# Splitting the weights of a two-layer encoder by DMA instead of on ScalarE and VectorE

## The chip, the cores and the metric

The kernel runs on one core of one Trainium2 chip. The metric is the device time of one execution in microseconds (us), the median of several runs. The engines are named as in the profile: PE is TensorE's matmul, PEld its weight load, DVE is VectorE, ACT is ScalarE, POOL is GpSimd, SP is SyncE. SPq, ACTq and POOLq are the instruction queues from which these three engines issue DMAs; q1 is the DMA queue that SP's transfers use and q0 the one that POOL's use.

## What is computed

Two request groups, 512 and 256 tokens of 1024 features in float32, go through the same two encoder layers:

```
n = rmsnorm(x)
q, k, v, xr, yr, g = split(n @ w_in)            # w_in is 1024 x 7168
att = rmsnorm(diff_attention(rope(norm(q)), rope(norm(k)), v))
rec = (scan_forward + scan_backward)(conv(xr)) * gelu(yr)
x   = x + (sig(g0) * (att @ w_a) + sig(g1) * (rec @ w_r)) @ w_out
x   = x + square(relu(rmsnorm(x) @ w_ff1)) @ w_ff2   # 1024 -> 4096 -> 1024
```

All products are wanted to float32 accuracy. TensorE takes the type float32r, which keeps the upper part of a float32. So each operand is split into an upper part hi (rounded to float32r) and a lower part lo = x - hi, and each product is three matmuls: hi by hi, hi by lo, lo by hi.

## The kernel before

The 768 tokens lie along the free axis, the features on the 128 partitions, 8 tiles of them. The weights come from HBM as 304 strips over the two layers: 288 of 128 x 1024 float32 (512 KB) and 16 of 128 x 512 (`rgw`, the gates of the recurrence). The list `plan` (from line 206) holds them in the order in which PE takes them. `prefetch(upto)` (line 225) issues for each strip of the plan a load on SP's queue into `raw` (2 buffers), then `split`: ACT rounds `raw` into `whi` (line 197) and DVE subtracts it into `wlo` (line 200). `whi` and `wlo` have WB = 4 buffers each. `wload` (line 239) hands PE its strip and has the strips up to AHEAD = 8 further on prefetched, as far as buffers allow.

The order of PE's instructions is the order of the program. For the other engines and the queues a planner fixes the order at build time: it places every instruction when its inputs and buffers are free by its own estimates. On the chip each engine and each queue then runs in that fixed order, so an instruction that waits holds up all that stand behind it.

A layer has four stages. In the attention stage (about 395 us) PE takes projections of q, k, v and a gate, 32 strips, and between their chunks, at places written out in the table STEPS, the steps of the 8 heads: transposes, scores, softmax on ACT and DVE, products with v. In the branch stages (`wa`, `wr`) the first four strips (NF = 4) are used together, feature tile by feature tile, in `first_strips`. Between them lies the recurrent stage, whose convolution and scans are ACT's and DVE's. The feed-forward stage (about 540 us) takes 64 strips one after the other.

POOL issues few transfers: stores of attention results (`ats`, line 634) and their loads (line 690), stores and loads of the branch sums (`ms`, lines 707 and 835), loads and stores of x (lines 856 and 925). It also adds the branch sums (line 842). The loads of x for layer 0 are issued on SP's queue (lines 371 and 373), between them the first two weight strips.

Of the kernel before, what the change touches and what calls it, by code (L numbers as in the profile page):

```python
# [9 lines left out]
F32 = mybir.dt.float32  # L10
F32R = mybir.dt.float32r
AF = mybir.ActivationFunctionType
ALU = mybir.AluOpType
# [16 lines left out]
AHEAD = 8  # strips of weights that are split ahead of their use  # L30
# attention: how many chunks of the other products (FILL, in this order) the tensor engine takes before each step of
# each of the 8 heads
# [23 lines left out]
# recurrent tiles in pairs: x: input and convolution, y: output gate, g: gates of the recurrence (tile, direction),  # L56
# s: scan, d: a strip of the branch's gate
# [6 lines left out]
WB = 4  # strips of split weights on chip  # L64

# columns of the packed per-feature vectors
V_N1, V_N2, V_BG, V_CW, V_CB, V_RB, V_RL, V_SG, V_GQ, V_GK, NV = 0, 8, 16, 32, 64, 72, 104, 120, 121, 122, 123
# columns of the vectors that every partition holds
# [4 lines left out]
def trunk_kernel(ctx: ExitStack, tc: tile.TileContext, xT, wqk, wv, wx, wy, wg0, wg1, wa, wr, wo, wf1, wf2,  # L73
# [10 lines left out]
    ident = cp.tile([P, P], F32, name="ident")  # L84
    make_identity(nc, ident)
    # the mean over D on every partition; over the 128 features of a head it is 8 times that
# [19 lines left out]
    def small_params(l, ap_):  # L106
        """per-layer scalars: -lam, 8 softplus(-L), folded gains, rotary tables."""
        v_ = vt[l]
        r_ = ap_.tile([P, NR], F32, name=f"rep{l}", tag="rep")
        nc.scalar.dma_start(out=r_, in_=rep[l])  # L110
        o = {}
        lam_init = 0.8 - 0.6 * math.exp(-0.3 * l)
        o["sg"] = tiny([P, 1], f"sg_{l}", "sg")
        V.tensor_scalar(out=o["sg"], in0=v_[:, V_SG:V_SG + 1], scalar1=-4.0 * (1.0 - lam_init), scalar2=0.0,
                        op0=ALU.mult, op1=ALU.add)
        o["gs"] = tiny([P, 1], f"gs_{l}", "gs")
        V.tensor_tensor(out=o["gs"], in0=v_[:, V_GQ:V_GQ + 1], in1=v_[:, V_GK:V_GK + 1], op=ALU.mult)
        # lam
        pr = tiny([P, 2, HD], f"lpr_{l}", "lpr")
        lv = r_[:, R_LV:R_LV + 256].rearrange("p (a b d) -> p a b d", a=2, b=2)  # L120
        V.tensor_tensor(out=pr, in0=lv[:, :, 0, :], in1=lv[:, :, 1, :], op=ALU.mult)
        ls = tiny([P, 2], f"ls_{l}", "ls")
        V.reduce_sum(out=ls, in_=pr, axis=AX)
        fn("ln_exp", ls, ls, AF.Exp)
        o["nlam"] = tiny([P, 1], f"nlam_{l}", "nlam")
        V.tensor_tensor(out=o["nlam"], in0=ls[:, 1:2], in1=ls[:, 0:1], op=ALU.subtract)
        V.tensor_scalar(out=o["nlam"], in0=o["nlam"], scalar1=1.0, scalar2=-lam_init, op0=ALU.mult, op1=ALU.add)
        # rotary tables with the gains: [P, NT, 4, ROT]
        o["t1"] = ap_.tile([P, NT, 4, ROT], F32, name=f"t1_{l}", tag="t1")
        o["t2"] = ap_.tile([P, NT, 4, ROT], F32, name=f"t2_{l}", tag="t2")  # L130
        for nm, c0, w in (("t1", R_GC, 0), ("t2", R_GS, 1)):
            V.tensor_tensor(
                out=o[nm], in0=rott[:, w].unsqueeze(2).to_broadcast([P, NT, 4, ROT]),
                in1=r_[:, c0:c0 + 64].rearrange("p (c d) -> p c d", c=4).unsqueeze(1).to_broadcast([P, NT, 4, ROT]),
                op=ALU.mult)
        # 8 softplus(-L) = 8 (max(-L, 0) + log1p(exp(-|L|)))
        L_ = v_[:, V_RL:V_RL + 16]
        mx = tiny([P, 16], f"spm_{l}", "spm")
        ng = tiny([P, 16], f"spn_{l}", "spn")
        V.tensor_scalar(out=ng, in0=L_, scalar1=-1.0, scalar2=0.0, op0=ALU.mult, op1=ALU.add)  # L140
        V.tensor_scalar(out=mx, in0=ng, scalar1=0.0, scalar2=0.0, op0=ALU.max, op1=ALU.add)
        e_ = tiny([P, 16], f"spe_{l}", "spe")
        V.tensor_tensor(out=e_, in0=L_, in1=ng, op=ALU.min)
        fn("ln_exp", e_, e_, AF.Exp)
        s_ = tiny([P, 16], f"sps_{l}", "sps")
        V.tensor_scalar(out=s_, in0=e_, scalar1=1.0, scalar2=2.0, op0=ALU.mult, op1=ALU.add)
        V.reciprocal(out=s_, in_=s_)
        V.tensor_tensor(out=s_, in0=s_, in1=e_, op=ALU.mult)
        s2 = tiny([P, 16], f"spq_{l}", "spq")
        V.tensor_tensor(out=s2, in0=s_, in1=s_, op=ALU.mult)  # L150
        pl = tiny([P, 16], f"spp_{l}", "spp")
        NS = 8
        V.tensor_scalar(out=pl, in0=s2, scalar1=1.0 / (2 * NS + 1), scalar2=1.0 / (2 * NS - 1), op0=ALU.mult, op1=ALU.add)
        for i in range(NS - 2, -1, -1):
            V.tensor_tensor(out=pl, in0=pl, in1=s2, op=ALU.mult)
            V.tensor_scalar(out=pl, in0=pl, scalar1=1.0, scalar2=1.0 / (2 * i + 1), op0=ALU.mult, op1=ALU.add)
        V.tensor_tensor(out=pl, in0=pl, in1=s_, op=ALU.mult)
        V.scalar_tensor_tensor(out=pl, in0=pl, scalar=2.0, in1=mx, op0=ALU.mult, op1=ALU.add)
        o["sp"] = tiny([P, 16], f"sp_{l}", "sp")
        o["nsp"] = tiny([P, 16], f"nsp_{l}", "nsp")  # L160
        V.tensor_scalar(out=o["sp"], in0=pl, scalar1=8.0, scalar2=0.0, op0=ALU.mult, op1=ALU.add)
        V.tensor_scalar(out=o["nsp"], in0=pl, scalar1=-8.0, scalar2=0.0, op0=ALU.mult, op1=ALU.add)
        return o

# [4 lines left out]
    def table(name):  # L169
        """what follows uses another table set of ScalarE than what came before: keep the two apart."""  # L170
# [23 lines left out]
    def split(hi, lo, src, eng="act"):  # L194
        """src (f32, SBUF) = hi + lo exactly."""
# [6 lines left out]
    # the weights in the order in which the tensor engine takes them; they are loaded and split ahead of it  # L202
# [22 lines left out]
    def prefetch(upto):  # L225
        while len(ready) < min(upto, len(plan)):
# [5 lines left out]
            raw = wp.tile([P, n], F32, tag="raw", name=nm("raw"), bufs=2)  # L232
            nc.sync.dma_start(out=raw, in_=src)
            hi = wp.tile([P, n], F32R, tag="whi", name=nm("whi"), bufs=WB)
            lo = wp.tile([P, n], F32R, tag="wlo", name=nm("wlo"), bufs=WB)
            split(hi, lo, raw)
# [10 lines left out]
    def mm3(ps, pairs):  # L247
        """pairs: (weight hi, weight lo, x hi, x lo) per k-tile; stationary is the first pair."""
# [6 lines left out]
    def strip(ps_pool, w, acts, g):  # L255
        """one strip of 128 output features for the tokens of group g."""
# [7 lines left out]
    def first_strips(ps_pool, name, l, acts):  # L264
        """the first strips of a branch side by side, k-tile by k-tile: the last tiles of acts come late"""
# [14 lines left out]
    def newton(vv, y, q, out=None, add=0.0, f=1.0):  # L280
        """y = ln(v / f + add) -> -2 f rsqrt(v / f + add) in out (q by default)."""
# [8 lines left out]
    def prep(xt, gm, nh, nl, g, k):  # L290
        """x * gain, split; the norm's factor is applied to the products."""
# [6 lines left out]
    def squares(xt, g, alloc, before=None):  # L298
        """sum over the feature tiles of x^2, split"""
# [16 lines left out]
    def stats(ss, rb, rtok, g, alloc, ps_pool, ptag, np_pool=None, ntag=None):  # L316
        """rb = -2 / rms of the tokens on every partition; rtok = 1 / rms with the tokens on partitions."""
# [23 lines left out]
    def scaled(out, ps, rb, g):  # L341
        """out = ps / rms"""
        off, n = GROUPS[g]
        V.scalar_tensor_tensor(out=out, in0=ps, scalar=-0.5, in1=rb[:, off:off + n], op0=ALU.mult, op1=ALU.mult)  # L344
# [7 lines left out]
    def norm1(l, xt, alloc):  # L352
        """splits x * gain for the two groups and sums the squares; the rest follows beside the first products"""
# [25 lines left out]
    for l in range(DEPTH):  # L379
        v_ = vt[l]  # L380
        # ================= attention =================
# [9 lines left out]
        def tok_proj(w, t, j, c):  # L391
            """token tile t, 256 columns of chunk c of w -> half a bank."""
# [14 lines left out]
        def proj_out(h, tp, ps, rtok):  # L407
            """the products of two token tiles, times 1 / rms; their squares per component"""
# [8 lines left out]
        def proj_close(h):  # L417
            """norms of q and k, rotary embedding"""
# [40 lines left out]
        def proj_first():  # L459
            """head 0, group A, k-tile by k-tile as the input comes"""  # L460
# [67 lines left out]
        def core(h):  # L528
            """steps of one head, each a function that issues one batch for the tensor engine and what follows it."""
# [3 lines left out]
            def tr_qk(g, w):  # L533
# [10 lines left out]
                # component c lies in the rows r; q's lower part and a second copy of k's upper part go to the rows o  # L544
# [14 lines left out]
            def score(qt):  # L559
# [8 lines left out]
                # (qh + ql) kh over all rows, qh kl over the half of the rows in which the component lies  # L568
# [20 lines left out]
            def tr_w(qp, kp):  # L589
                """qp: pair of query tiles (0, 1 of group A; 2 of B); kp: pair of key tiles"""  # L590
# [59 lines left out]
        # the norm's factors are worked out while the first products run  # L650
# [32 lines left out]
        # ================= attention branch =================  # L683
# [26 lines left out]
        # ================= RG-LRU =================  # L710
# [9 lines left out]
        def rg_x(j):  # L720
            """input of the recurrence: product, convolution, split"""
# [95 lines left out]
        # ================= recurrent branch, merge =================  # L817
# [34 lines left out]
        # ================= output projection =================  # L852
# [21 lines left out]
        # ================= feed-forward =================  # L874
# [8 lines left out]
        for c in range(NC_):  # L883
# [10 lines left out]
            for s, g in order:  # L894
# [3 lines left out]
                if c == 0 and s < 2:  # L898
                    # the norm's factors come while the first two strips run
# [32 lines left out]
        # the pools of this half are closed before the next layer's attention opens its own  # L932
# [80 lines left out]
```

## Time and profile before

| | us |
|---|---|
| median of 3 runs (2759.18 to 2762.40) | 2761.06 |
| span of the profiled execution | 2757.5 |
| PE busy in it | 2727.5 (99%) |
| PEld busy | 2430.3 (88%) |
| DVE busy | 1638.4 (59%) |
| ACT busy | 1323.3 (48%) |
| POOL busy | 96.5 (3%) |

The profiled execution gives its own time as the span, from the first to the last instruction; the median lies 3.6 us above it. Matmuls overlap in the records, so the mean duration of a matmul is longer than the time between two of them. An engine's busy share is a mean over stages with different limits.

### The profile page before, as it was taken

How to read it: one execution, taken by the hardware profiler on the slowest of the kernel's cores; microseconds unless marked ns; L12 is line 12 of the kernel's file. 1: busy time of each engine (PE TensorE's matmuls, PEld its weight loads, DVE VectorE, ACT ScalarE, POOL GpSimd, SP SyncE). 2: the span in 40 equal slices, each digit the busy share in tenths (PEclk: the TensorE clock that was granted, in tenths of full speed). 3: DMA queues.
4: the chain of work that ended last, by engine and by line, in shares of the span. 5: the costliest groups of instructions: out<-in, count | busy, mean ns of one | idle time of the engine just before them, and what ended most of it. 6: DMA issues, size and time to landing. Idle time of an engine off the chain costs nothing.

```text
span 2757.5 us, 41112 instructions
## 1 busy us (share of the span) xinstructions
PE 2727.5 (99%) x16840; PEld 2430.3 (88%) x16840; DVE 1638.4 (59%) x2966; ACT 1323.3 (48%) x2293; POOL 96.5 (3%) x134
## 2 busy tenths in 40 slices
PE   8999999999999999999999999999999999999999
PEld 8899888888888888888898988888888888888888
DVE  8777873697645444444567778637985454444443
ACT  7777871568324222222467778716683242222221
POOL 0000000000120000000100000000002100000000
PEclk9999999999999999999999999999999999999999
DMA  3111123122331111111321111231213222112111
GB/s 129 53 49 54 44 86 122 60 65 69 117 103 65 62 62 66 65 62 62 103 69 45 46 57 45 98 107 54 73 64 141 80 66 65 62 62 69 62 62 69
DMA packets 57485, 199.36 MB, mean 72 GB/s; under 512 B 7504, under 2 KB 9936, under 8 KB 57296
## 3 DMA queue, kind: packets, MB, share of 16 engines
q1 hardware_dynamic: 48384, 161.50, 17.9%
q0 software_dynamic: 8192, 34.61, 3.5%
q8 instruction: 132, 2.16, 0.3%
q10 hardware_dynamic: 720, 0.62, 0.1%
q14 instruction: 57, 0.47, 0.1%
HBM read 177.83 MB, written 18.87 MB: 71 GB/s over the span
## 4 chain that ended last, share of the span: by engine, by line
PE 87%; DVE 6%; ACT 5%; issue 1%; DMA 0%; ACTq 0%; DVEq 0%
PE d L251 19%; PE d L252 19%; PE d L253 19%; PE d L398 4%; PE d L399 4%; PE d L397 4%; PE s L571 3%; PE d L276 2%; PE d L275 2%; PE d L277 2%; PE d L520 2%; PE d L522 2%; PE d L521 1%; DVE t L806 1%; PE t L595 1%
## 5 line engine op out<-in xcount | busy, mean ns | idle before, releaser
L197 ACT ACTIVATE whi<-raw 128x1024 fp32r<-128x1024 f32 (+1 forms) x304 | 315.0, 1037 | 773.2 <-PE d L252 627.3
L200 DVE TENSOR_TENSOR wlo<-raw,whi 128x1024 fp32r<-128x1024 f32 (+1 forms) x304 | 371.1, 1222 | 125.4 <-ACT whi L197 124.9
L252 PE MATMUL d<-n2l,whi 128*128 128x512 f32 (+1 forms) x1024 | 344.8, 337 | 0.0
L251 PE MATMUL d<-n2h,whi 128*128 128x512 f32 (+1 forms) x1024 | 344.5, 336 | 0.0
L253 PE MATMUL d<-n2h,wlo 128*128 128x512 f32 (+1 forms) x1024 | 344.1, 336 | 0.0
L252 PE MATMUL d<-sX,whi 128*128 128x512 f32 (+1 forms) x704 | 237.0, 337 | 0.0
L251 PE MATMUL d<-sY,whi 128*128 128x512 f32 (+1 forms) x640 | 215.4, 337 | 0.2 <-DVE rec L344 0.2
L253 PE MATMUL d<-sY,wlo 128*128 128x512 f32 (+1 forms) x640 | 215.1, 336 | 0.0
L251 PEld LDWEIGHTS d<-n2h,whi 128*128 128x128 f32 x1024 | 194.4, 190 | 20.8
L253 PEld LDWEIGHTS d<-n2h,wlo 128*128 128x128 f32 x1024 | 194.2, 190 | 20.5
L252 PEld LDWEIGHTS d<-n2l,whi 128*128 128x128 f32 x1024 | 194.4, 190 | 20.1
L908 ACT ACTIVATE fr<-fr 128x512 f32<-128x512 f32 (+1 forms) x128 | 65.9, 515 | 270.5 <-DVE fr L907 270.5
L907 DVE SCALAR_TENSOR_TENSOR fr<-d,rb 128x512 f32<-128x512 f32 (+1 forms) x128 | 71.4, 558 | 176.6 <-PE d L253 168.9
L252 PE MATMUL d<-hl,whi 128*128 128x256 f32 (+1 forms) x512 | 172.4, 337 | 0.0
L251 PE MATMUL d<-hh,whi 128*128 128x256 f32 (+1 forms) x512 | 172.3, 336 | 0.0
L253 PE MATMUL d<-hh,wlo 128*128 128x256 f32 (+1 forms) x512 | 172.0, 336 | 0.0
L922 DVE TENSOR_TENSOR sZ<-sZ,d 128x256 f32<-128x256 f32 (+1 forms) x128 | 71.0, 555 | 141.6 <-PE d L253 141.6
L251 PE MATMUL d<-sZ,whi 128*128 128x512 f32 (+1 forms) x448 | 150.8, 337 | 0.2 <-DVE rec L344 0.2
L252 PE MATMUL d<-sZ,whi 128*128 128x512 f32 (+1 forms) x448 | 150.7, 336 | 0.0
L253 PE MATMUL d<-sZ,wlo 128*128 128x512 f32 (+1 forms) x448 | 150.6, 336 | 0.0
L397 PE MATMUL d<-whi,sZ 128*128 128x256 f32 x512 | 148.7, 290 | 0.0
L397 PE MATMUL d<-whi,sY 128*128 128x256 f32 x512 | 148.0, 289 | 0.0
(310 smaller groups left out, 7348.2 us busy)
## 6 DMA issues: line engine op xcount, KB each, us to landing
raw<-wf SPq DMA_DIRECT2D x128, 512.0 KB, 3.3
raw<-wqk SPq DMA_DIRECT2D x32, 512.0 KB, 3.4
raw<-wg SPq DMA_DIRECT2D x32, 512.0 KB, 3.3
raw<-wv SPq DMA_DIRECT2D x16, 512.0 KB, 4.0
raw<-wa SPq DMA_DIRECT2D x16, 512.0 KB, 4.1
raw<-wx SPq DMA_DIRECT2D x16, 512.0 KB, 3.4
raw<-wy SPq DMA_DIRECT2D x16, 512.0 KB, 3.3
raw<-wr SPq DMA_DIRECT2D x16, 512.0 KB, 3.6
```

What stands on the lines that cost most here:

```text
L197: S.activation(hi, src, AF.Copy)
L200: V.tensor_tensor(out=lo, in0=src, in1=hi.bitcast(F32), op=ALU.subtract)
L251: PE.matmul(ps, lhsT=wh, rhs=xh, start=(k == 0), stop=False)
L252: PE.matmul(ps, lhsT=wh, rhs=xl, start=False, stop=False)
L253: PE.matmul(ps, lhsT=wl, rhs=xh, start=False, stop=(k == n - 1))
L397: PE.matmul(j, lhsT=xh, rhs=hi[:, kk], start=(k == 0), stop=False)
L398: PE.matmul(j, lhsT=xh, rhs=lo[:, kk], start=False, stop=False)
L399: PE.matmul(j, lhsT=xl, rhs=hi[:, kk], start=False, stop=(k == 7))
L571: PE.matmul(pss[c], lhsT=z["q"][r, c, qs], rhs=z["kl"][r, off:off + n] if x else z["k"][:, c, off:off + n], start=(x == c), stop=(x != c))
L907: V.scalar_tensor_tensor(out=r_, in0=ps, scalar=0.0, in1=rb2[:, off:off + n], op0=ALU.max, op1=ALU.mult)
L908: S.activation(r_, r_, AF.Square, scale=0.5)
L922: V.tensor_tensor(out=xg, in0=xg, in1=ps, op=ALU.add)
```

## The change

The raw strips are no longer loaded. POOL issues a load of the strip straight into the float32r buffer `whi`, which converts on the way. ACT copies `whi` times -1 into `wlo`. POOL then issues a second load of the same strip from HBM that adds onto what `wlo` holds, so that it ends as w - hi. WB goes from 4 to 5. All else in the diff is removed comments.

```diff
-WB = 4  # strips of split weights on chip
+WB = 5
...
             n = src.shape[1]
-            raw = wp.tile([P, n], F32, tag="raw", name=nm("raw"), bufs=2)
-            nc.sync.dma_start(out=raw, in_=src)
+
             hi = wp.tile([P, n], F32R, tag="whi", name=nm("whi"), bufs=WB)
             lo = wp.tile([P, n], F32R, tag="wlo", name=nm("wlo"), bufs=WB)
-            split(hi, lo, raw)
+            G.dma_start(out=hi, in_=src)
+            S.activation(lo, hi.bitcast(F32), AF.Copy, scale=-1.0)
+            G.dma_start(out=lo, in_=src, accum_op=ALU.add)
             ready.append((hi, lo))
```

## Rows read from the trace of the kernel before

**Rows 1.** The page, span, busy time of engines, and DMA queues (packets, MB, share).

```profile
span 2757.5 us, 41112 instructions
PE 2727.5 (99%) x16840; PEld 2430.3 (88%) x16840; DVE 1638.4 (59%) x2966; ACT 1323.3 (48%) x2293; POOL 96.5 (3%) x134
...
q1 hardware_dynamic: 48384, 161.50, 17.9%
```

**Rows 2.** Busy time by stretch: PE, PEld, DVE, ACT, POOL, clock, DMA share, GB/s.

```profile
0.00:25.00 25.00, 16.65 (x111) 16.07 (x112) 19.67 (x46) 19.97 (x38) 0.70 (x6) 1.00 0.67 228
25.00:420.00 395.00, 386.36 (x2786) 350.63 (x2786) 308.19 (x730) 303.27 (x639) 13.19 (x24) 1.00 0.19 62
...
820.00:1376.00 556.00, 556.00 (x3206) 492.23 (x3205) 247.23 (x371) 159.61 (x245) 6.53 (x12) 1.00 0.20 67
...
1450.00:1840.00 390.00, 381.95 (x2625) 342.48 (x2624) 278.32 (x631) 272.01 (x560) 16.29 (x30) 0.99 0.20 66
```

**Rows 3.** The page's costliest groups, the two that split the weights.

```profile
L197 ACT ACTIVATE whi<-raw 128x1024 fp32r<-128x1024 f32 (+1 forms) x304 | 315.0, 1037 | 773.2 <-PE d L252 627.3
L200 DVE TENSOR_TENSOR wlo<-raw,whi 128x1024 fp32r<-128x1024 f32 (+1 forms) x304 | 371.1, 1222 | 125.4 <-ACT whi L197 124.9
```

**Rows 4.** Timeline of ACT in the feed-forward stage of layer 0.

```profile
915.12 1.06 ACT L197 ACTIVATE whi<-raw 128x1024 fp32r<-128x1024 f32 x1 [7.28 <-PE d L252]
...
923.46 1.06 ACT L197 ACTIVATE whi<-raw 128x1024 fp32r<-128x1024 f32 x1 [0.73 <-PE d L252]
...
929.77 0.63 ACT L908 ACTIVATE fr<-fr 128x512 f32<-128x512 f32 x1 [4.50 <-DVE fr L907]
```

**Rows 5.** DMA issues: engine, count, KB each, median us from issue to landing.

```profile
raw<-wf SPq DMA_DIRECT2D x128, 512.0 KB, 3.3
...
raw<-wr SPq DMA_DIRECT2D x16, 512.0 KB, 3.6
...
sY<-xT POOLq DMA_DIRECT2D x8, 384.0 KB, 6.9
```

**Rows 6.** Groups of POOL: busy us, mean ns, idle before them and its releasers.

```profile
L634 POOL DMA_DIRECT2D ats<-at x32 | 17.5, 547 | 780.2 <-DVE rc L583 468.8 <-DVE at L633 252.1 <-DVE rc L582 51.0
L842 POOL TENSOR_TENSOR m<-m,sX 128x768 f32<-128x768 f32 x8 | 17.5, 2183 | 38.1 <-DVE sX L841 33.1 <-DMA m<-ms 5.0
...
L925 POOL DMA_DIRECT2D xs<-sY x16 | 8.7, 544 | 591.5 <-DVE sY L922 591.5
```

**Rows 7.** Timeline of the start, from the first weight load to its first use.

```profile
0.74 0.39 SPq L233 DMA_DIRECT2D raw<-wqk  x1
...
1.02 0.29 POOL masks.py:199 TENSOR_SCALAR_AFFINE_SELECT ident<-ident 128x128 f32<-128x128 f32 x1
...
5.67 1.04 ACT L197 ACTIVATE whi<-raw 128x1024 fp32r<-128x1024 f32 x1
...
7.57 1.22 DVE L200 TENSOR_TENSOR wlo<-raw,whi 128x1024 fp32r<-128x1024 f32 x1
...
8.84 0.58 PE L472 MATMUL d<-wlo,sY 128*128 128x256 f32 x1 [0.90 <-DVE wlo L200]
```

**Rows 8.** Busy time in the start's second stretch, columns as in Rows 2.

```profile
8.00:16.00 8.00, 7.07 (x35) 6.78 (x36) 8.00 (x13) 8.00 (x14) 0.00 (x0) 1.00 1.01 338
```

**Rows 9.** Timeline of ACT behind the first four strips of wr.

```profile
744.01 2.11 ACT L197 ACTIVATE whi<-raw 128x1024 fp32r<-128x1024 f32 x2 [27.10 <-issue]
...
751.19 1.06 ACT L197 ACTIVATE whi<-raw 128x1024 fp32r<-128x1024 f32 x1 [3.56 <-DMA raw<-wr]
```

**Rows 10.** Timeline of PE there: the start of the strip after next.

```profile
755.88 0.40 PE L251 MATMUL d<-rch,whi 128*128 128x512 f32 x1
```

**Rows 11.** Waits of PE in 24 to 420 us: us, times, longest.

```profile
PE t L543 <- DVE q L551: 4.2, 5, 1.8
PE s L571 <- DVE kl L555: 1.6, 1, 1.6
```

**Rows 12.** Groups of DVE in 25 to 420 us, the weight split.

```profile
L200 DVE TENSOR_TENSOR wlo<-raw,whi 128x1024 fp32r<-128x1024 f32 x32 | 39.0, 1223 | 8.5 <-ACT whi L197 8.5
```

## Prediction

> **What bounds the kernel now.** I read the busy times first. PE is busy for 2727.5 of 2757.5 us [rows 1], so only 30 us exist in which it does nothing, and no edit that leaves the matmuls alone can win more than that. Then the stretches: 8.4 us of the 30 lie in the first 25, where the first data come; 8.6 in the attention stage of layer 0 and 8.1 in that of layer 1; none in the feed-forward stage [rows 2]. About 3 us are the last sum and store, which nothing here touches. Last I looked at who ends PE's waits in the attention stage: mostly DVE, which has not yet written the split queries or keys [rows 11]. The weight split itself is almost never waited for: in the feed-forward stage ACT stands 7.28 us until PE frees a buffer, and a strip is wanted every 8.34 us (915.12 to 923.46) [rows 4]. So the supply of weights has slack, and the question is what the change does to that slack, to the start and to the 17 us of attention.
>
> **What it removes.** 304 subtractions on DVE, 371.1 us [rows 3]. DVE is not the bound, so this counts only where PE waits for DVE. In the attention stage the 32 subtractions are 39.0 us [rows 12] of 308.2, so DVE's load falls from 78% to 68% of the stretch [rows 2]. At least, the waits don't shrink; at most, all 16.7 us of the two stages go. Waits in proportion to the removed work would lose 39.0/308.2 = 13%, or 2 us. I take -2, the end nearer to a row.
>
> **What stays.** ACT still makes 304 passes of the same shape: 1037 ns [rows 3], now `wlo` from `whi`. What changes is what they wait for: before, a buffer, with the raw strip long there; now the landing of a load that could only be issued once that buffer was free.
>
> **What it adds.** 608 issues on POOL's queue in place of 304 on SP's. A POOL issue took 547 ns beside a DVE at 78%, and 544 in the feed-forward stage [rows 6]; 608 x 0.55 = 333 us of 2757, spread. No row shows a casting or an accumulating load. A plain strip lands in 3.3 us, and POOL's slowest loads, eight of 384 KB at once, in 6.9 [rows 5]. I bound both new loads by these, 3.3 to 6.9, and take 3.6 for the casting load, which moves the same bytes as `raw<-wr`, and the middle, 5, for the adding one, with both ends kept. One strip then needs 3.6 + 1.06 + 5 = 9.7 us from free buffer to ready (8.0 to 14.9), where it needed 1.04 + 1.22 = 2.3. Is that covered? In the feed-forward stage five buffers give a strip four strips of time, 4 x 8.34 = 33 us, less 9.7: 24 us to spare, against 3 x 8.34 - 2.3 = 23 before. So nothing there: the fifth buffer pays for the longer chain. POOL runs in order, so strip i+1's casting load stands behind strip i's adding load, which waits for ACT: 0.55 + 3.6 + 1.06 + 0.55 = 5.8 us a strip, under 8.34. In the attention stage a strip lasts 395/32 = 12.3 us, and weight loads stand in one queue with the stores of `ats`. Those stood 780.2/32 = 24 us each [rows 6], with nothing behind them. A load planned behind a store waits only as long as the plan errs; with two strips of time ahead, 24.7 us, less 9.7, an error under 15 us is hidden. I cost it at nothing.
>
> Of the transfer itself: 161.5 MB took 17.9% of 2757.5 us on q1 [rows 1], which is 327 GB/s and 1.6 us of all 16 engines for a strip. The page "Collectives: The Full Stack" of the Trainium skill, section "The bandwidth ceiling", says that an adding transfer is slower than a copy not for the addition but because it reads two sources. No row here shows one; by that page the adding load would hold the engines an estimated 3.2 us, the pair 4.8 of 8.34, and the sum below would stay as it is.
>
> **The start.** The first `wlo` was ready at 8.79 and PE took it at 8.84 [rows 7]. Now POOL issues the first casting load, behind its work on `ident`, at 1.3 instead of 0.74, so it lands at about 6.2 instead of 5.67. ACT's pass ends at 7.3, and the adding load lands 3.3 to 6.9 later, at 10.6 to 14.2, in a stretch in which x fills the DMA engines (share 1.01) [rows 8]. PE's second matmul slips by 1.8 to 5.4 us, and all behind it with it, since PE stays busy afterwards. SP's loads of x come sooner without weights between them, which helps nothing while `wlo` is late. I take +4.
>
> **The joints.** Behind the four strips that are used together, four buffers come free within about 3 us. Strip 4 lies in the fifth buffer now. Strip 5 can start when strip 0 is done, about 744.0 [rows 9], and PE wants it at 755.88 [rows 10]: 11.9 us, against a chain of 9.7 (8.0 to 14.9, and 17.1 with one POOL addition of 2.18 [rows 6] ahead in the queue). That costs 0 to 5.2 us at each of four exits, and the same bounds hold at the four entries: 0 to 42 in all. At 9.7 all fit barely; I take +2 for the few that don't.
>
> **Sum.** -2 + 4 + 2 = +4, so a span of 2761.5; with the 3.6 us by which the median lies above the profiled span, 2765. What a measurement of this kernel can tell from no change is 0.2%, 5.5 us: 2755.5 to 2766.6. The forecast is no change, on its slow side, with a range of its own from 2754 to 2774.
>
> **Rivals.**
>
> (a) *The relief of DVE counts in full.* PE's waits in the attention stage end mostly with DVE [rows 11]. If a tenth less load ends nearly all of them, 16.7 us go; with +4 at the start this is 2748. For it: the releasers named. Against it: the steps stand in a fixed order around the old split, and ACT's passes now depend on transfers.
>
> (b) *ACT stands before the landing in the attention stage*: the slower side. ACT is in order. If the planner puts the pass where it believes the casting load to have landed, and it lands later, softmax and the emptying of PE's sums wait too. ACT is idle for 395 - 303.3 = 91.7 us in this stretch [rows 2], 2.87 us for each of 32 strips. From a mean wait of 2.87 on PE is held. In one place where ACT waited for a strip that had just been requested it stood 3.56 us [rows 9]: 64 x (3.56 - 2.87) = 44 us, so 2809. For it: this row. Against it: the plan knows of a transfer's delay, and only its error counts.
>
> (c) *The pair of transfers becomes the bound.* It decides once casting and adding hold the DMA engines for more than 8.34 us a strip, with 1.6 for the first from 6.7 us for the second, four times a plain load. At six times, 9.6: 128 feed-forward strips x (11.2 - 8.34) = 366 us, so about 3130. For it: nothing shows the rate. Against it: the plain rate leaves a factor of four.
>
> (d) *POOL's issues stretch.* The Trainium skill's page "SBUF — State Buffer", section "Who interferes with whom", says that a DVE instruction in a two-port mode shuts GpSimd out of SBUF, descriptor writing included; that speaks against moving weights to POOL. As a mechanism of this kernel: each issue grows by a DVE instruction of up to 1.22 us [rows 3], the chain by 2.4, and the eight joints pay about 2.4 each, 19 us: 2784. The rows speak against it: 547 ns beside a busy DVE, 544 beside a quiet one [rows 6].
>
> (e) *It doesn't do what it says*: if the casting load didn't round, the adding load would leave zeros. The instructions and their times would be the same; this lies within the forecast.
>
> **Chances.** Forecast 0.47 (with e), (a) 0.25, (b) 0.17, (c) 0.08, (d) 0.03. The range from 2747 to 2809 leaves out a part of (a), the upper half of (b), and (c): about 0.2. Faster by over 0.2%: (a) and a little of the forecast's low end, 0.27. Within: 0.36. Slower: 0.09 of the forecast, (b), (c) and (d), 0.37.
>
> **What would show it.** In the changed profile: DVE's busy time near 1270; 608 more issues on POOL near 0.55 us; the landing of both loads between 3.3 and 6.9; PE's first matmul with `wlo` at 10.6 to 14.2; PE without a gap in the feed-forward stage; at the joints waits of PE for `wlo`, now released by a DMA, of a few us; in the attention stage PE idle near 8 us a layer. Wrong would be: an adding load far beyond 6.9 us; waits of ACT at the new pass for a DMA that sum to over 90 us in one attention stage; a clearly smaller or larger idle time of PE there.

## The result, and the profile after

The changed kernel takes 2856.3 us (median of 4 runs, 2854.47 to 2861.53) against 2761.06: the ratio is 1.035, with an interval of 1.034 to 1.037. It is 95 us slower, and the range ended at 2809. The page after, spans, busy times and the queue that now carries the weights (MB, share of 16 engines), against [rows 1]:

```profile
span 2855.5 us, 41175 instructions
...
PE 2754.5 (96%) x16840; PEld 2442.1 (86%) x16840; DVE 1298.3 (45%) x2662; ACT 1331.9 (47%) x2293; POOL 524.4 (18%) x742
...
q0 software_dynamic: 95744, 345.03, 51.9%
```

The removed work did go: DVE lost 340 us. But PE, whose matmuls are the same, now idles 101 us (2855.5 less 2754.5) where it idled 30, and is busy 27 us longer. The second follows from the first, as the windows show (columns as in [rows 2]):

```profile
0.00:25.00 25.00, 8.27 (x47) 8.01 (x48) 14.18 (x32) 18.56 (x33) 7.11 (x15) 1.00 0.91 260
25.00:420.00 395.00, 377.62 (x2729) 340.91 (x2728) 267.68 (x694) 292.96 (x628) 51.80 (x76) 0.99 0.41 93
...
770.00:830.00 60.00, 51.56 (x271) 43.49 (x270) 20.18 (x26) 15.40 (x17) 29.70 (x30) 0.90 0.69 173
...
830.00:1390.00 560.00, 559.89 (x3219) 495.18 (x3218) 156.89 (x288) 151.20 (x229) 94.06 (x133) 1.00 0.56 126
...
1390.00:1480.00 90.00, 80.94 (x571) 76.61 (x570) 41.46 (x94) 43.63 (x88) 21.63 (x34) 0.94 0.57 139
```

Where PE stood, its granted clock was lower afterwards: a mean of 0.90 in 770 to 830 and 0.94 in 1390 to 1480, so part of the time at 1.2 and not 2.4 GHz. A gap costs more than its own length. The feed-forward stage is as full as before.

PE runs the same 16840 matmuls in the same order in every kernel here. So the start of matmul number n can be set against its start before, and the slip over a stage is what the stage lost, its slower clock included. This ledger (us lost against the kernel before, worked out from all matmul starts, layer 0 / layer 1; `wo` is the output projection) is used below:

```
run                     start  attention    wa branch   recurrent   wr branch   wo           feed-fwd  sum
changed                  +8.3  +11.7/+25.1  +0.7/+1.0   +1.8/+3.2   +7.5/+10.4  +13.0/+14.8  +0.4/0.0   98.0
e1_six_four              +6.7  +1.6/-0.6    +12.7/+12.8 -0.9/-0.9   +9.5/+9.8   +14.3/+15.8  0/0        80.7
e2_light_second_load     +6.6  +11.3/+15.0  +0.1/+0.8   -0.9/-0.9   +0.2/+2.4   +9.5/+10.2   0/0        54.4
e3_plain_on_SP           +6.7  +12.6/+18.8  +2.5/+7.1   +1.3/+1.1   +10.9/+9.0  +10.2/+10.6  +5.5/+3.2  99.5
e4_both                  +6.6  +2.5/-1.5    +17.0/+20.3 -0.9/-0.9   +15.3/+15.5 +7.9/+7.5    0/0        89.3
e5_six_five              +8.7  +2.9/+0.4    +4.3/+5.1   -0.7/-0.9   -0.5/-0.5   +20.5/+19.6  0/0        59.1
e6_sums_off_POOL         +7.5  +4.3/+0.6    +2.4/+5.3   -0.9/-0.9   -0.5/-0.5   0.0/0.0      0/0        17.4
e7_first_strips_old_way  +0.8  +3.8/+1.9    +4.6/+6.3   -0.9/-0.6   -0.5/-0.5   +20.2/+19.2  0/0        54.3
e10_sum_on_VectorE_only  +8.1  +3.6/+1.0    +4.3/+4.8   -0.9/+0.4   -0.5/-0.5   +9.8/+9.2    0/0        39.4
e11_all_cures            +1.0  +1.0/+1.4    0.0/0.0     -0.7/-0.3   -0.5/-0.5   0.0/0.0      0/0         1.4
e12_sums_off_five_five   +7.1  +12.1/+20.4  +1.7/+1.4   +3.0/+4.4   +10.4/+10.9 +6.5/+5.2    +3.8/+8.1  95.1
```

Five things make up the 98 us: 8 at the start, 26 in the attention stages proper, 11 at the start of layer 1 (counted in its attention), 18 in the `wr` branches and 28 at `wo`. The last 7 are small.

**How the two loads interlock.** The groups of the new pass and of the adding load, the landing of both loads in the feed-forward stage (us), and the largest waits (us, times, longest):

```profile
L236 ACT ACTIVATE wlo<-whi 128x1024 fp32r<-128x1024 f32 (+1 forms) x304 | 314.9, 1036 | 1096.9 <-DMA whi<-wf 642.9
...
L237 POOL DMA_DIRECT2D wlo<-wf x128 | 111.1, 868 | 855.8 <-ACT wlo L236 809.6
```

```profile
whi<-wf POOLq DMA_DIRECT2D x128, 512.0 KB, 6.1
wlo<-wf POOLq DMA_DIRECT2D x128, 512.0 KB, 5.4
```

```profile
POOL wlo L237 <- ACT wlo L236: 1378.4, 269, 9.0
ACT wlo L236 <- DMA whi<-wf: 642.9, 121, 9.5
```

Before, ACT's pass waited for PE to free a buffer [rows 3]; now it waits for a landing, and POOL waits for ACT, 269 times. POOL in the feed-forward stage shows why:

```profile
1041.00 0.86 POOL L237 DMA_DIRECT2D wlo<-wf  x1 [7.08 <-ACT wlo L236]
1041.71 0.70 POOL L235 DMA_DIRECT2D whi<-wf  x1
1049.25 0.87 POOL L237 DMA_DIRECT2D wlo<-wf  x1 [6.85 <-ACT wlo L236]
```

The casting load of the next strip is issued right behind the adding load of this one. The two overlap on the queue q0. The casting load lands after 6.1 us, where 3.5 are enough when no adding load stands right ahead of it (run e1 below); then ACT passes, and only then can POOL go on. One round takes 8.2 us (1041.00 to 1049.25), just under the 8.34 in which PE takes a strip. So this stage loses nothing, but the supply has almost no reserve left: it gains 0.1 us a strip on PE, and a strip that comes late is hardly made up for.

**The start.** The timeline of ACT's first pass, POOL's adding load and PE's first use of it:

```profile
7.40 1.06 ACT L236 ACTIVATE wlo<-whi 128x1024 fp32r<-128x1024 f32 x1 [2.34 <-DMA whi<-wqk]
...
8.77 0.89 POOL L237 DMA_DIRECT2D wlo<-wqk  x1 [6.39 <-ACT wlo L236]
...
17.28 0.58 PE L473 MATMUL d<-wlo,sY 128*128 128x256 f32 x1 [9.22 <-DMA wlo<-wqk]
```

The adding load took some 8.5 us from issue to use, beside the loads of x (DMA share 0.91).

**The start of layer 1.** Here ACT and DVE also normalize the new x, and POOL also stores it, in the same queue. ACT's passes and the work behind the last of them, then DVE's and PE's part:

```profile
1409.02 1.06 ACT L236 ACTIVATE wlo<-whi 128x1024 fp32r<-128x1024 f32 x1 [4.47 <-PE d L254]
...
1420.17 1.06 ACT L236 ACTIVATE wlo<-whi 128x1024 fp32r<-128x1024 f32 x1 [5.02 <-DMA whi<-wqk]
...
1431.31 1.06 ACT L236 ACTIVATE wlo<-whi 128x1024 fp32r<-128x1024 f32 x1 [5.02 <-DMA whi<-wqk]
1432.28 0.71 ACT L295 ACTIVATE sZ<-sY,vec 128x512 fp32r<-128x512 f32 x1
```

```profile
1433.02 0.75 DVE L296 SCALAR_TENSOR_TENSOR sX<-sY,vec,sZ 128x512 fp32r<-128x512 f32 x1 [5.61 <-ACT sZ L295]
1433.69 0.68 DVE L923 TENSOR_TENSOR sY<-sY,d 128x512 f32<-128x512 f32 x1
...
1434.42 0.58 PE L472 MATMUL d<-whi,sZ 128*128 128x256 f32 x1 [8.45 <-DVE sY L923]
```

ACT stands 5 us before each landing, with the normalization queued behind it; DVE stands 5.61 us for that, and the sum that empties PE's bank (L923) is queued behind on DVE. So PE stands 8.45 us. The profile names DVE, the last link; the first is `whi<-wqk`. A round is 11.1 us, longer than a strip's 8.34. POOL's queue has a part in it: the adding load was issued at 1410.38 and the next casting load only at 1413.83, behind two stores of x that waited for DVE's sums.

**Attention and wo.** In attention the pass is moved rather than waited for. An example is the timeline of ACT at one head's start, with PE's wait there. Before, two passes ran ahead of the head's first copy of q (L550):

```profile
270.94 1.06 ACT L197 ACTIVATE whi<-raw 128x1024 fp32r<-128x1024 f32 x1
...
272.29 1.05 ACT L197 ACTIVATE whi<-raw 128x1024 fp32r<-128x1024 f32 x1
...
273.95 0.59 ACT L550 ACTIVATE q<-t 64x512 fp32r<-64x512 f32 x1
...
281.74 0.66 PE L543 MATMUL t<-ident,qk 128*128 128x128 f32 x2 [1.77 <-DVE q L551]
```

After the change they run behind it:

```profile
285.13 0.58 ACT L551 ACTIVATE q<-t 64x512 fp32r<-64x512 f32 x1
...
287.00 1.06 ACT L236 ACTIVATE wlo<-whi 128x1024 fp32r<-128x1024 f32 x1 [0.76 <-DMA whi<-wv]
288.08 0.59 ACT L551 ACTIVATE q<-t 64x512 fp32r<-64x512 f32 x1
...
289.67 1.06 ACT L236 ACTIVATE wlo<-whi 128x1024 fp32r<-128x1024 f32 x1
...
294.72 0.41 PE L544 MATMUL t<-ident,qk 128*128 128x128 f32 x2 [3.53 <-DVE q L552]
```

The passes fall among the copies of q, and PE's transposes stood 3.53 us there instead of 1.77. This one place is 1.8 us; that the rest of layer 0's 11.7 has the same form is argued from it and not shown place by place. At `wo`, POOL's sums, the loads of `m` and the weight issues take turns:

```profile
802.88 1.84 POOL L843 TENSOR_TENSOR m<-m,sX 128x768 f32<-128x768 f32 x1 [2.19 <-DMA m<-ms]
805.51 0.90 POOL L237 DMA_DIRECT2D wlo<-wo  x1 [0.78 <-ACT wlo L236]
806.53 2.09 POOL L843 TENSOR_TENSOR m<-m,sX 128x768 f32<-128x768 f32 x1
808.57 0.59 POOL L836 DMA_DIRECT2D m<-ms  x1
809.15 0.55 POOL L235 DMA_DIRECT2D whi<-wo  x1
...
820.20 0.55 POOL L235 DMA_DIRECT2D whi<-wo  x1
```

PE's waits in both layers (us, times, longest) tell the `wr` branches and `wo` apart:

```profile
PE d L278 <- DMA wlo<-wr: 12.9, 3, 6.2
...
PE d L252 <- ACT sX L197: 7.6, 2, 3.8
...
PE d L252 <- ACT sZ L197: 5.6, 2, 3.8
```

In the `wr` branches they end with the landing of an adding load. At `wo` they end with ACT's split of a branch sum (`sZ` in layer 0, `sX` in layer 1): PE stands there for a sum that came late through POOL's queue, and not for a strip.

### The profile page after: what moved, and what is told of

Its sections match the earlier page's. It is cut to its first block, busy times and chain, and to the rows that moved or that the text cites. A ratio compares the mean times of both kernels' runs of the same rounds, so it can differ in the third digit from the quotient of the medians.

```text
span 2855.5 us, 41175 instructions
## 1 busy us (share of the span) xinstructions
PE 2754.5 (96%) x16840; PEld 2442.1 (86%) x16840; DVE 1298.3 (45%) x2662; ACT 1331.9 (47%) x2293; POOL 524.4 (18%) x742
## 3 DMA queue, kind: packets, MB, share of 16 engines
q0 software_dynamic: 95744, 345.03, 51.9%
## 4 chain that ended last, share of the span: by engine, by line
issue 52%; PE 31%; POOL 10%; DMA 3%; ACT 2%; DVE 1%; POOLq 0%; ACTq 0%
PE d L253 9%; PE d L254 9%; PE d L252 9%; POOL wlo L237 5%; POOL whi L235 4%; DMA whi<-wo 1%; DMA whi<-wqk 1%; PE d L277 1%; PE d L278 1%; PE d L276 1%; POOL ats L635 1%; POOL m L843 0%; ACT wlo L236 0%; DMA af<-ats 0%; ACT L188 0%
## 5 line engine op out<-in xcount | busy, mean ns | idle before, releaser
L236 ACT ACTIVATE wlo<-whi 128x1024 fp32r<-128x1024 f32 (+1 forms) x304 | 314.9, 1036 | 1096.9 <-DMA whi<-wf 642.9
L237 POOL DMA_DIRECT2D wlo<-wf x128 | 111.1, 868 | 855.8 <-ACT wlo L236 809.6
L923 DVE TENSOR_TENSOR sZ<-sZ,d 128x256 f32<-128x256 f32 (+1 forms) x128 | 71.0, 554 | 178.4 <-PE d L254 178.3
L253 PEld LDWEIGHTS d<-sX,whi 128*128 128x128 f32 x704 | 134.0, 190 | 18.0 <-DVE sX L200 4.2
```

What stands on the lines that cost most here:

```text
L236: S.activation(lo, hi.bitcast(F32), AF.Copy, scale=-1.0)
L237: G.dma_start(out=lo, in_=src, accum_op=ALU.add)
L253: PE.matmul(ps, lhsT=wh, rhs=xl, start=False, stop=False)
L923: V.tensor_tensor(out=xg, in0=xg, in1=ps, op=ALU.add)
```

## The experiments

**Six upper buffers, four lower (e1).** With six upper and four lower buffers the casting load of a strip is released two strips earlier than its adding load, and no longer by the same matmul.

```diff
-  hi = wp.tile(..., tag="whi", bufs=WB)
-  lo = wp.tile(..., tag="wlo", bufs=WB)
+  hi = wp.tile(..., tag="whi", bufs=WB + 1)
+  lo = wp.tile(..., tag="wlo", bufs=WB - 1)
```

> The casting load gets 6 buffers, the lower part 4, in place of 5 and 5; bytes, transfers and passes are the same. On POOL's queue each casting load then stands two strips ahead of the adding load that it stood just behind. Theory Q (the queue): casting load, ACT's pass and adding load are one chain per strip on an in-order queue, 6.1 + 1.04 + 0.9 = 8.1 us against 8.34 us of a strip, and over it wherever something else stands between. With the casting load landed long before ACT's pass the chain is gone: POOL's wait for ACT before the adding load falls from 1378 us to under 500, the 10 us at the second layer's start and most of the 29 us at the two output projections go, the 8 us of the first strip stay: 2790 (2775 to 2810). Rival W (the weight): the adding load keeps the 16 engines busy about twice as long as a plain one and everything lands late for that; nothing changes: 2850 to 2862.

2844.5 us, ratio 1.030 [1.029, 1.032], outside both ranges. The loss in both attention stages and at the start of layer 1 is gone (+1.6/-0.6), `whi<-wf` lands in 3.5 us, and POOL's waits for ACT fell from 1378.4 to 214.2 us. The `wa` branches, with four lower buffers, lost 12.7 each, which hides the gain in the total, and `wo` kept its loss, against Theory Q. The order of the casting load is the cause in attention; the time by itself would not have shown it. At the head shown above, both passes run ahead of the first copy of q again:

```profile
278.91 1.06 ACT L236 ACTIVATE wlo<-whi 128x1024 fp32r<-128x1024 f32 x1
280.25 1.06 ACT L236 ACTIVATE wlo<-whi 128x1024 fp32r<-128x1024 f32 x1
...
281.91 0.59 ACT L551 ACTIVATE q<-t 64x512 fp32r<-64x512 f32 x1
```

So the edit changes the landing and the place of ACT's pass together, and what each gives is not told apart.

**A light second load (e2).** The second load overwrites instead of adding.

```diff
-  G.dma_start(out=lo, in_=src, accum_op=ALU.add)
+  G.dma_start(out=lo, in_=src)
```

> The second load is a plain one: it overwrites the negative in place of being added to it, so the lower parts are wrong. Order, queue and waits are those of the changed kernel; only the weight of the transfer goes. Theory W: with half the engine time of the second load most of the loss goes: 2775 (2765 to 2790). Theory Q: the chain is still there and only shorter, about 4.5 + 1.04 + 0.7 = 6.2 us a strip; the feed-forward stage gets slack, but the second layer's start and the output projections, where POOL stands for other things, keep about half of their loss: 2810 (2795 to 2830).

2816.3 us, ratio 1.020 [1.019, 1.022], in the range of Theory Q and not of W. The weight of the addition is 44 of the 98 us, above all in the `wr` branches (15), in layer 1's attention with its start (10) and at `wo` (8); attention in layer 0 keeps its loss. The page and the landing time:

```profile
q0 software_dynamic: 95744, 345.03, 39.7%
...
wlo<-wf POOLq DMA_DIRECT2D x128, 512.0 KB, 3.5
```

39.7% of a span of 2811.8 us against 51.9% of 2855.5 is 1116 against 1482 us; without the 3.5% (97 us) that q0 already carried, a plain strip holds the engines 1.68 us ((1116 - 97)/608) and an adding one 2.88 (means over the 304 strips, 16 of them of half size). The Trainium skill's page "Collectives: The Full Stack", section "The bandwidth ceiling", says of ReduceScatter, a collective that adds, that it is slower because the add needs two source reads; carried over to this load, that is an estimated 3.2 us. The trace agrees in direction, with 2.88.

**Plain transfers on SP (e3).** Six lines of stores and loads leave POOL's queue; one stands for all.

```diff
-  G.dma_start(out=ats[h][:, off:off + n], in_=at)
+  nc.sync.dma_start(out=ats[h][:, off:off + n], in_=at)
```

> The six kinds of plain transfers (attention results, branch sums, x) are issued on SP's queue, which the change left empty; POOL keeps the weight loads and the 16 additions. Theory Q: what stood in POOL's queue between the weight loads goes, so the period at the second layer's start falls from 11.15 us a strip to about 9 and the joints lose less, while the chain of 8.1 us itself stays: 2830 (2815 to 2845). Theory W: the bytes are the same: 2850 to 2862.

2858.6 us, ratio 1.036 [1.034, 1.037], the number of Theory W. Nothing is gained in the total: in the ledger what `wo` (7) and layer 1's attention (6) get back turns up in `wa` and in the feed-forward stage. To take the stores out of the queue doesn't pay while the two weight loads hold each other.

**Both edits (e4).** The two diffs above together.

> 6 and 4 buffers, and the plain transfers on SP's queue. Theory Q: 2782 (2770 to 2800): what stays is the first strip's 8 us and a part of the attention stage's 25. Theory W: 2850 to 2862.

2850.9 us, ratio 1.033 [1.031, 1.034], in the range of Theory W. Attention as in e1, but `wa` (17.0/20.3) and `wr` (15 each) are worse: with four lower buffers, PE's waits there end with the landing of adding loads. Why these come later than in e1 was not tried.

**Six and five (e5).** Against e1 the lower parts get their fifth buffer back. The recurrent stage's scratch goes from 2 buffers to 1 to make room.

```diff
-  lo = wp.tile(..., tag="wlo", bufs=WB - 1)
+  lo = wp.tile(..., tag="wlo", bufs=WB)
...
-  ac = rp.tile(..., tag="sq", bufs=2)
+  ac = rp.tile(..., tag="sq", bufs=1)
```

> 6 buffers for the upper and 5 for the lower parts. The 4 KB come from one scratch buffer of the recurrent stage (sq, 2 to 1) and a small tile. Against the kernel before, 6 and 4 lost 0 to 2 us in each attention stage, where the change lost 12 and 25, but 13 at each wa joint, where the change lost 1. Theory L (lower buffers): the four strips used together then held all four lower buffers, so the fifth adding load could not start; with five the wa loss goes back to 1 to 2 and the attention stages stay at 0 to 2: about 2812 (2800 to 2825). Rival P (place): with its casting load two strips ahead every adding load stands behind more transfers on the same rings, wherever many are wanted at once: wa stays at 10 to 13, 2838 (2830 to 2848).

2817.9 us, ratio 1.021 [1.019, 1.022], in the range of Theory L. Attention +2.9/+0.4, `wr` -0.5 each, `wa` 4 to 5 (Theory L had 1 to 2), `wo` +20 each, more than in the changed kernel. At the start of layer 1 ACT's passes come every 8.34 us and wait for PE again, which is full there:

```profile
1392.59 1.06 ACT L236 ACTIVATE wlo<-whi 128x1024 fp32r<-128x1024 f32 x1 [0.47 <-PE d L254]
...
1400.93 1.06 ACT L236 ACTIVATE wlo<-whi 128x1024 fp32r<-128x1024 f32 x1 [0.48 <-PE d L254]
```

```profile
1390.00:1480.00 90.00, 90.00 (x674) 85.39 (x673) 54.00 (x128) 55.10 (x116) 22.42 (x35) 1.00 0.60 145
```

**The sums off POOL (e6).** On top of six and five, the branch sum goes to DVE, the loads of `m` and of x in the merge to SP.

```diff
-  G.dma_start(out=m, in_=ms[j])
+  nc.sync.dma_start(out=m, in_=ms[j])
...
-  G.tensor_tensor(out=m, in0=m, in1=sg, op=ALU.add)
+  V.tensor_tensor(out=m, in0=m, in1=sg, op=ALU.add)
...
-  G.dma_start(out=t_, in_=xT[k] if l == 0 else xs[k])
+  nc.sync.dma_start(out=t_, in_=xT[k] if l == 0 else xs[k])
```

> As the one with 6 and 5 buffers, and the addition of the branch sums on VectorE, the loads of the sums and of x on SP's queue. Theory Q at the output projections (13 to 15 us lost each): the sums stand behind weight loads and behind POOL's waits for ACT; off POOL the loss falls to 5 or less, total about 2792 (2782 to 2802). Rival W: the transfers of the sums share the engines with adding loads that hold them twice as long, on whichever queue: the loss stays above 10, 2812.

2778.0 us, ratio 1.006 [1.005, 1.008], below even Theory Q's range. `wo` loses nothing: in e5 its 20 us in each layer came from POOL's other work there.

**The first strips the old way (e7).** Six and five, and the first four strips are loaded raw by SP and split by ACT and DVE.

```diff
+  if len(ready) < 4:
+      raw = e0.tile([P, n], F32, tag="raw", name=nm("raw"), bufs=2)
+      nc.sync.dma_start(out=raw, in_=src)
+      split(hi, lo, raw)
+      ready.append((hi, lo))
+      continue
```

> As the one with 6 and 5 buffers, but the first four strips of the program are loaded raw on SP's queue between the loads of x and split by ACT and DVE, as before the change. Theory S: the 7 to 8 us of the start are the adding load of strip 0, which stands behind the loads of x; they go, the rest stays: 7 less than with 6 and 5 buffers. Rival: PE's start is held by the loads of x themselves, whatever splits the weights: 2 less at most.

2811.9 us, ratio 1.019 [1.017, 1.020]. The start's loss goes from 8.7 to 0.8 us, as Theory S has it; some 4 us of it come back in attention and `wa`.

**The subtraction on POOL (e8).** The kernel before, with DVE relieved by POOL.

```diff
-  split(hi, lo, raw)
+  S.activation(hi, raw, AF.Copy)
+  G.tensor_tensor(out=lo, in0=raw, in1=hi.bitcast(F32), op=ALU.subtract)
```

> The kernel before with one edit: POOL and not DVE subtracts the upper part from the raw strip (about 2.9 us each by POOL's 128x768 additions of 2.18 us). It relieves DVE as the change did, without any other load. If the relief is worth what DVE's place as releaser of PE's waits suggests, up to 16 us go: 2748. Theory: it is worth next to nothing, since with 6 and 4 buffers and the same relief the attention stages ended level with before (+1.6 and -0.6 us): 2757 to 2765.

2879.9 us, ratio 1.043 [1.042, 1.045], far outside both forecasts. It says nothing on DVE's relief, since DVE itself slowed down. POOL's group, and then one of DVE's (ns min/median/max), whose median was 556 in the kernel before:

```profile
L237 POOL TENSOR_TENSOR wlo<-raw,whi 128x1024 fp32r<-128x1024 f32 (+1 forms) x304 | 722.1, 2379 | 1523.3 <-ACT whi L236 1469.6
```

```profile
L200 DVE TENSOR_TENSOR hl<-fr,hh x64: 692/1330/1967, 987.9 to 2846.1; 128x512 fp32r<-128x512 f32 x32, 128x256 fp32r<-128x256 f32 x32
```

**A constant lower part (e9).** The cleaner form of the same question: no subtraction, and nothing in its place.

```diff
+  low = cp.tile([P, 1024], F32R, name="low")
+  V.memset(low.bitcast(F32), 2.0 ** -10)
...
-  lo = wp.tile([P, n], F32R, tag="wlo", name=nm("wlo"), bufs=WB)
-  split(hi, lo, raw)
-  ready.append((hi, lo))
+  S.activation(hi, raw, AF.Copy)
+  ready.append((hi, low[:, :n]))
```

> The kernel before with one change: all lower parts of the weights are one constant tile, written once, so the 304 subtractions on VectorE and their buffers are gone and nothing is added on any queue. This leaves the lower parts of the weights out of the product (a constant stands for them); every matmul stays. It measures by itself what the relief of VectorE is worth. Theory R0 (the relief is worth nothing; PE's waits in the attention stages are for the chain of one head's steps and not for VectorE's load): 2755 to 2762 us, attention stages within 2 us each of before, at most the start shorter by 1 to 2. Rival R1 (a tenth less load ends PE's waits in the attention stages, as rival (a) of the prediction has it): about 2745 us, attention stages 8 us shorter each.

2768.0 us, ratio 1.003 [1.002, 1.004]. Neither number was met, for a reason outside the question: the feed-forward matmuls took longer, 4.7 us a layer. The attention window, against [rows 2], answers the question itself:

```profile
25.00:420.00 395.00, 384.32 (x2789) 346.97 (x2789) 271.75 (x681) 304.13 (x641) 13.14 (x24) 1.00 0.18 61
```

DVE's load fell by 36 us (308.19 to 271.75), and PE idles 10.7 us where it idled 8.6. So the relief doesn't shorten PE's waits as a whole. The slip over the stage is -2.5 us in layer 0 and about nothing in layer 1. PE's matmuls and not its waits are shorter there (386.36 us busy before, 384.32 here); why was not tried.

**Only the sum on DVE (e10).** Six and five, with the loads left on POOL.

```diff
-  G.tensor_tensor(out=m, in0=m, in1=sg, op=ALU.add)
+  V.tensor_tensor(out=m, in0=m, in1=sg, op=ALU.add)
```

> Six upper and five lower buffers as in the run six_five, and only the branch sum moved from POOL to VectorE; the loads of m and of x in the merge stay on POOL's queue. Of the run six_five, wo lost 20 us a layer, and moving sum and loads together took this away. Theory P (POOL's sum itself, about 2 us standing behind its m, holds the weight issues behind it): wo loses at most 5 us a layer, time about 2783. Rival L (the loads of m stand in POOL's queue behind adding loads that wait for ACT, land late, and the merge is late by them): wo still loses 12 us or more a layer, time 2805 or more.

2798.3 us, ratio 1.014 [1.012, 1.015], midway between the two theories: `wo` loses 9.8/9.2 instead of 20. Both parts count. The waits in 735 to 850 show the second:

```profile
DVE m L843 <- DMA m<-ms: 16.4, 5, 8.9
...
POOL m L836 <- DVE ml L200: 6.1, 2, 5.6
```

POOL stands with a load of `m`, whose buffer is not free, and weight issues stand behind it; the `m` so loaded comes late to DVE.

**The sums off POOL, at five and five (e12).** The three lines of e6 in the changed kernel itself.

> The changed kernel with its five and five buffers; only the branch sum moves to VectorE and the loads of m and x in the merge to SP. If wo's loss is POOL's other work alone, whatever the buffers: wo goes from +13.0 and +14.8 to about 0, the rest stays, so 2856 less 28, about 2828. Rival (with the casting load behind the adding load the lead at wo is short in any case): wo keeps 8 us or more a layer, 2840 or more.

2854.3 us, ratio 1.035 [1.033, 1.036]. 28 us were to go, and 3 went in the ledger. That is the rival's total, though `wo` fell further than the rival had it, to 6.5/5.2: the feed-forward stage now loses 3.8/8.1 and the `wr` branches 3 more. With the two loads interlocked, a strip that is late stays late, wherever the first delay is taken away. Of the edits that leave the loads as they are, only the casting load ahead makes the others pay.

**All cures (e11).** Six and five, sums off POOL, first strips the old way, and the loads of the attention output on SP:

```diff
-  G.dma_start(out=af, in_=ats[k])
+  nc.sync.dma_start(out=af, in_=ats[k])
```

> The changed way with each located loss taken out: six upper and five lower buffers, branch sum on VectorE, loads of m, of x and of the attention output in the merge on SP, and the first four strips loaded raw on SP and split by ACT and VectorE as before. If the stages add up as the ledger has it: 2778 of the run sums_off_POOL, less 7 of the start, less 2 to 6 of the attention branch's joints: 2764 to 2771, level with the kernel before to 0.3%, not faster. Rival (the relief of VectorE shows once nothing else is late): 2750 or less. Rival (the cures get into each other's way on SP's queue): 2775 or more.

2763.1 us (11 runs) against 2760.2 (18 runs), ratio 1.001 [1.000, 1.002]; both rivals are out. All stages are level with before to 1.4 us, and the cures together take back 96.6 of the 98.0 us. DVE is relieved in it too, and no stage gains more than 0.7 us. No version beat the kernel before.

## Why the prediction was wrong

**The failed step is the chain costed at nothing.** It had strip i+1's casting load behind strip i's adding load, "which waits for ACT: 0.55 + 3.6 + 1.06 + 0.55 = 5.8 us a strip, under 8.34", and "the fifth buffer pays for the longer chain". The order was right, its price was not. A casting load issued right behind an adding load lands in 6.1 us, not 3.6, and the round is 8.2, not 5.8. That held in the feed-forward stage. Elsewhere ACT and POOL have other work in the same round: 11.1 us at the start of layer 1, and 11.1 at `wo` (casting issues at 809.15 and 820.20), where it is the sums in the same queue that PE stands for. In attention the prediction hid errors of the plan behind two strips of lead; ACT's pass fell among the heads' steps all the same. A fifth buffer on both sides leaves both loads of a strip waiting for the same matmul; a sixth upper one breaks this (e1, e5), and without it neither e3 nor e12 paid.

**Joints, +2.** The bounds allowed 42 for entries and exits; measured are 18 in the `wr` branches (15 of them gone in e2, all in e5) and 28 at `wo` (gone in e6), 46 in all. A POOL addition ahead in the queue was in the bounds, at 2.18 us each; that loads of `m` hold POOL, that the sums themselves come late to PE, and that a loss there can hardly be caught up, was not. The chain's lower end, 8.0 us, has 3.6 for the casting load where the bound is 3.3; with that it is 7.7, which changes nothing.

**Start, +4.** Right in kind, measured 8.3. The adding load was bounded by 6.9 us; in the stretch with the loads of x it took 8.5. e7 gives 7.9 of it back.

**DVE's relief, -2.** No run shows a gain of that kind: with a tenth less load on DVE, PE's idle time in the attention stage does not fall (e9), and no stage gains more than 0.7 us (e11). The 2.5 us of layer 0 in e9 are near the forecast and not in the waits that it meant. PE's waits end with DVE [rows 11], but not for DVE's load; that they are for a step that a head's chain of steps brings late fits this and was not tested by itself. So rival (a) falls.

**The rivals on the slow side.** (b) had the right engine and landing, and its 44 us are near the 37 of attention with layer 1's start. That nearness is luck: its sign, waits of ACT of over 90 us in a stage, is absent: ACT has the pass later, among the head's steps, and its waits for each kind of strip sum to 6.2 us at most in layer 0's attention (33 to 430). (c) is out, q0 at 51.9%. (d) is out: the adding load's issue takes 0.87 us in the feed-forward stage and 0.87 to 0.88 in attention, where DVE is far busier, and a plain load in its place takes 0.53 (e2). The page that it rests on, the Trainium skill's "SBUF — State Buffer", section "Who interferes with whom", also says that a DVE operation with two inputs in SBUF contends with a GpSimd instruction that reads SBUF, and there e8's 1330 ns against 556 agrees. DVE's `fr<-d,rb`, whose input `d` lies in PSUM, took 558 ns in both.

The PE clock was in no term: 27 of the 98 us are PE's longer busy time after gaps. Of the signs that the prediction named, the landings between 3.3 and 6.9 us (medians of 5.4 and 6.1 in the feed-forward stage) and the full feed-forward stage came true; the first `wlo` was used at 17.28 us and not by 14.2, and PE's idle time in layer 0's attention stage rose from 8.6 to 17.4 us.

## What to carry to other kernels

When work moves from an engine to a queue, ask not only whether the round trip fits into a period but who else stands in that round on each in-order queue, and whether the supply can still get ahead after a delay. Give the first of two dependent loads a buffer more than the second, so that it is not released by the same event. Book losses by stage: e1 moved the total by 12 us and yet showed 36 us cured in attention and 24 made anew in `wa`.

## What was not expected of the hardware

An adding load of a strip from HBM holds the DMA engines 2.88 us against 1.68 for a plain one (means over the 304 strips), lands in 5.4 us against 3.5, and its issue on POOL takes 0.87 us against 0.53 (e2). A casting load lands like a plain one (3.5 to 3.6 us when it isn't behind an adding one). With one constant tile as the lower part, the feed-forward matmuls on it took 176.9 ns to the start of the next one instead of 173.4 (means over the 1024 of layer 0, from the matmul starts), at a granted clock of 0.998; why was not tried.
